# Zero-padding the rotary keys so that a 64-partition score product runs on 128

## The chip, the cores and the metric

The kernel runs on one core of a Trainium2 chip, in one launch. The metric is device time in microseconds. TensorE (PE) multiplies, with a load of its weights for each product (PEld); VectorE (DVE), ScalarE (ACT) and GpSimd (POOL) do the elementwise work, and SyncE (SP) issues most DMAs.

## What is computed

A diffusion backbone of two layers, each with a half-step feed-forward block, token mixing, and a second half-step block. Token mixing adds an mLSTM and a latent attention. The tokens are 256 of context and 256 latent ones. The attention has 8 heads; a head's queries and keys are a part of 128 columns without position and a rotary part of 64 columns, whose keys all heads share. Cut to that:

```
k_rope = _rope(z['a_kr'][:, :, None, :], cos, sin)
k = concatenate([k_nope, broadcast_to(k_rope, (B, T, A_HEADS, A_ROPE))], axis=-1)
q = concatenate([q_nope, _rope(q_rope, cos, sin)], axis=-1)

s = einsum('bqhd,bkhd->bhqk', q, k) * (128 + 64) ** -0.5
pr = softmax(s, axis=-1)
o = einsum('bhqk,bkhd->bqhd', pr, v)
```

Context queries see the 256 context keys; latent queries see all 512. In the last layer only latent queries are computed.

## The kernel before

All tensors lie with features on partitions and tokens along columns. Each operand of a large product is held as two parts, hi (the value in a rounded form, made by ACT) and lo (the rest, made by DVE), and a product is three: hi by hi, lo by hi, hi by lo. Weights come by DMA on SP as units of up to 1024 columns (`unit`), which ACT and DVE split into such parts.

Token mixing is `mix(l, after)`. The program order is written by generators: `mla()` yields between the steps of the attention, `mlstm()` between those of the other mixer, and a `Feed` puts steps of other products between them and draws the elementwise chains an operation at a time (`pump`). The framework's scheduler then sets the final order on each engine and picks which of the 56 work buffers of the pool `act` each tile gets.

The rotary keys are made once per layer, ahead of the attention: 64 rows are copied twice into the tile `krz`, once to each half of the partitions; `rope_gen` rotates the latent columns in place, and `split_gen` makes `kr`, a pair of tiles hi and lo over 128 partitions and 512 columns. For the queries, `head_parts` makes per head one tile over 128 partitions: the head's own half holds the hi part, the other half the lo part.

`scores(p, hd, s)` in `mla()` makes two blocks of scores (`sc`) for pair p, head hd of the pair and stream s, each of five products in one group (L1159). The first three are on the 128 columns without position. The fourth takes the query tile over 128 partitions with `kr[0]`, so hi and lo of the queries meet the keys' hi part in one product. The fifth takes the keys' lo part and must meet only the hi part of the queries, so both operands are cut to the head's own 64 partitions:

```
rp = slice(64 * hd, 64 * hd + 64)
steps = [(qh, kh), (ql, kh), (qh, kl), (qr[hd], kr[0]), (qr[hd][rp], kr[1][rp])]
```

Behind the scores come a maximum (`mx`, DVE L1163), an exponential and a scaling (`pr`, ACT L1168 and L1172), the transposes (`pT`, PE L1182), their split, and the product with the values (`ho`). There are 16 such jobs in layer 0 and 8 in layer 1. The scores' maxima share DVE with the gate chain of the mLSTM, the splitting of weights (`wl`, L226) and the convolution's taps. The taps read tiles `cpd`, whose edges POOL sets to zero (L684, L685).

Of the kernel before, what the change touches and what calls it, by code (L numbers as in the profile page):

```python
# [8 lines left out]
F32 = mybir.dt.float32  # L9
F32R = mybir.dt.float32r  # L10
# [6 lines left out]
P = 128  # L17
# [106 lines left out]
def body(ctx, tc, A):  # L124
# [29 lines left out]
    def put_aside():  # L154
        """The residual leaves its room to the token mixing, which needs it only at its end."""
        for j in range(KB):
            nc.sync.dma_start(aside[:, j, :], xs[j])
# [31 lines left out]
    def pair(n):  # L189
        """Room for the two parts of an operand of n columns."""  # L190
        if n <= HALF:
            t = act(F32R, "hl")
            return t[:, :n], t[:, HALF : HALF + n]
        return act(F32R, "hi")[:, :n], act(F32R, "lo")[:, :n]

    def split(src, n, hi_lo=None, scale=None):
        """src, or scale * src, as two parts."""
        hi, lo = pair(n) if hi_lo is None else hi_lo
        if scale is None:
            S.activation(hi, src, AF.Copy)  # L200
            V.tensor_tensor(lo, src, hi.bitcast(F32), ALU.subtract)
        else:
            S.activation(hi, src, AF.Copy, scale=scale)
            V.scalar_tensor_tensor(lo, src, scale, hi.bitcast(F32), ALU.mult, ALU.subtract)
        return hi, lo
# [5 lines left out]
    def load(dst, src):  # L211
        """On the SP queue, and at the start behind what the first norm needs."""
        with tc.issue_after(behind.pop(0)) if behind else nullcontext():
            nc.sync.dma_start(dst, src)
# [15 lines left out]
    def units(keys, n, kb):  # L230
        """A weight cut along its rows: a list of (hi, lo) [P, N] blocks."""
        res = []
        for key in keys:
            hi, lo = unit(key, n, kb)
            for k in range(kb):
                res.append((hi[:, k, :], lo[:, k, :]))
        return res

    def mm3(ps, lhs, rhs, lsl=slice(None), rsl=slice(None), late=False):
        """late: the second parts of rhs come last, as they are not there yet."""  # L240
        n = len(lhs)
        steps = [(k, *p) for k in range(n) for p in ((0, 0), (1, 0), (0, 1))]
        if late:
            steps.sort(key=lambda t: t[2])
        for i, (k, a, b) in enumerate(steps):
            TE.matmul(ps, lhs[k][a][:, lsl], rhs[k][b][:, rsl], start=i == 0, stop=i == 3 * n - 1)  # L246

    def mmu(parts, keys, n, kb, rhs, flip=False, turns=True):
        """Several products with one weight, cut along its rows into units: each
        unit serves all products before the next one is needed. parts: (out, slice  # L250
        of the unit's columns or of rhs' columns when flip, whether it is the first
        one of its bank: those of one bank form one group, as its first product clears
        the bank's marks). turns: the products take turns, block by block."""
        k0, nk = 0, len(rhs)
        for key in keys:
            hi, lo = unit(key, n, kb)
            order = [(k, i) for k in range(kb) for i in range(len(parts))]
            if not turns:
                order.sort(key=lambda t: t[1])
            for _, group in groupby(order, lambda t: t[0] if turns else 0):  # L260
                for k, i in group:
                    ps, sl, fresh = parts[i]
                    end = i + 1 == len(parts) or parts[i + 1][2]
                    (a, al), (b, bl) = (hi[:, k, :], lo[:, k, :]), rhs[k0 + k]
                    if flip:
                        (a, al), (b, bl) = (b[:, sl], bl[:, sl]), (a, al)
                    else:
                        a, al = a[:, sl], al[:, sl]
                    first, final_ = fresh and k0 + k == 0, end and k0 + k == nk - 1
                    TE.matmul(ps, a, b, start=first, stop=False)  # L270
                    TE.matmul(ps, a, bl, start=False, stop=False)  # L271
                    TE.matmul(ps, al, b, start=False, stop=final_)  # L272
                yield
            k0 += kb
# [5 lines left out]
    # The engine holds one set of functions at a time: Tanh is in one, Ln in another,  # L280
    # Exp in both.
# [12 lines left out]
    def tanh_half(out, src):  # L294
        """2 sigmoid(x) - 1"""
        held[0] = "tanh"
        S.activation(out, src, AF.Tanh, scale=0.5)

    def silu2(out, src):
        """2 x sigmoid(x)"""  # L300
        tanh_half(out, src)
        V.scalar_tensor_tensor(out, out, 1.0, src, ALU.add, ALU.mult)

# [7 lines left out]
    def silu_rows():  # L311
        """Twice the silu of the two conditioning vectors on every partition, in halves."""
# [9 lines left out]
    def ada_first():  # L322
        """Shift and scale of the first norm, before anything else can run."""
        # both parts of both vectors side by side, as one operand of four columns
# [67 lines left out]
    class Ada:  # L392
        """Modulation blocks, fed into other work; loads run some blocks ahead."""
# [10 lines left out]
        def run(self, frac):  # L404
            """Until this share of the blocks is done."""
# [15 lines left out]
    def newton(r, ss, n, width, t=None):  # L421
        """One step that takes r = rsqrt(ss / width + EPS) to float32's accuracy."""
# [5 lines left out]
    def rstd_of(sq_sum, n, width):  # L428
        """sq_sum: to be summed over the partitions, and over its list."""
# [10 lines left out]
    class Norm:  # L440
        """Sum of squares over the blocks of one stream, added as they come."""
# [32 lines left out]
    def flush():  # L474
        """The norm that a stream still lacks."""
        while pending:
            pending.pop()()
# [5 lines left out]
    def last_blocks(make, rhs, streams, l, g, norms, norm, tail=2):  # L483
        """The 8 output blocks of a product added to the residual; the last ones (tail) by
        streams, so that a stream's norm runs beside the other's products."""
# [89 lines left out]
    def mix(l, after):  # L575
# [12 lines left out]
        class Feed:  # L588
            """Work that stands between the steps of the attentions, whose steps wait
            for each other: products that need no other result soon (step), and the  # L590
            elementwise chains behind them, an operation at a time (pump)."""
# [28 lines left out]
            def advance(self, i):  # L620
                """One step of this item; whether it had one left."""
# [12 lines left out]
            def step(self, n=1, open_=lambda key: True):  # L634
                """n steps of the first items that there is room for."""
# [19 lines left out]
        # two blocks of the queries' width: a bank each, or one for both  # L655
# [13 lines left out]
        def split_gen(jobs, scale=None):  # L669
            """jobs: (source, hi, lo)."""  # L670
# [10 lines left out]
        def conv_start(ps):  # L681
            """The tokens of two segments, each between zeros."""
# [6 lines left out]
        def conv_gen(jobs, scale):  # L689
            """Three taps along the tokens, then silu, then the two parts. jobs: (padded  # L690
            tokens, first weight's column by segment, hi, lo)."""
# [24 lines left out]
        def gate_rows():  # L716
            """Gates of all heads and directions as rows: head h forward at h, backward
            at 32 + h; and what the exponents need of them."""
# [8 lines left out]
        def gate_chain(f, i_, e):  # L727
            rows = lambda t, a=0, b=36: t[a:b, :T]
            yield from log_sigm(rows(f), rows(e))
            # parts that are multiples of 2^-12 add without rounding; the rest is small  # L730
# [52 lines left out]
            # minus the stabiliser, exactly, and its parts for the product that spreads it  # L783
# [17 lines left out]
        def gate_cols():  # L801
            """As columns of tokens."""
# [17 lines left out]
        def log_sigm(f, e):  # L820
            """f becomes log sigmoid(f)."""
# [9 lines left out]
        # latent projections of the attention  # L831
# [22 lines left out]
        def rope_gen(z, c0, then):  # L854
            """In place on the latent columns of z, which start at c0; then the parts."""
# [13 lines left out]
        def head_parts(z, dst):  # L869
            """By head: both parts of the queries one over the other, as the rows of one product."""  # L870
# [40 lines left out]
        def gate2(key, keys, name):  # L911
            """2 sigmoid - 1 of two blocks."""
# [24 lines left out]
        class Head:  # L937
# [97 lines left out]
            def scale(self):  # L1035
# [5 lines left out]
                # a first rsqrt from the bits, then to float32's accuracy  # L1041
# [11 lines left out]
            def turn(self):  # L1053
                """Back to columns of tokens, times the output gate."""
# [91 lines left out]
        def mla():  # L1146
            def scores(p, hd, s):
# [3 lines left out]
                rp = slice(64 * hd, 64 * hd + 64)  # L1151
                (qh, ql), (kh, kl) = qn_[hd], kn[hd]
                steps = [(qh, kh), (ql, kh), (qh, kl), (qr[hd], kr[0]), (qr[hd][rp], kr[1][rp])]
# [88 lines left out]
        kr = pair(T)  # L1242
        rope = rope_gen(z, HALF, split_gen([(z, *kr)]))
# [31 lines left out]
        # merge  # L1275
# [57 lines left out]
def _pack(I):  # L1333
# [65 lines left out]
    # constants of the shapes alone  # L1399
# [36 lines left out]
```

## Time and profile before

| | before |
|---|---|
| median of 3 runs | 2396.31 us (2394.90 to 2396.78) |
| span of the profiled execution, core 0 | 2395.4 us |
| PE busy | 2352.9 us (98%) |
| DVE busy | 1601.3 us (67%) |
| ACT busy | 990.7 us (41%) |
| POOL busy | 171.9 us (7%) |
| HBM traffic | 131 GB/s over the span |

The page gives the profiled execution by its span, from the first to the last instruction; what lies around it is what the times of the runs have beyond that, at most 1.4 us here. PE is busy nearly throughout, but its busy time is a sum over stretches of different kinds, and starts and ends must be read in the rows: matmuls overlap, and their ends are modelled. A start-to-start distance is the time that a product takes in the row of products.

### The profile page before, as it was taken

The page shows a single profiled execution, that of the slowest core. Times are in us where ns is not written, and L with a number is a line of the kernel's source. Part 1 is how long each engine was busy: PE and PEld are TensorE (multiplying, and loading weights), DVE is VectorE, ACT ScalarE, POOL GpSimd, SP SyncE. Part 2 cuts the span into 40 slices and gives each one's busy share as a digit, 9 for nine tenths or more (in the row PEclk, how much of TensorE's full clock was granted, in tenths as well). Part 3 has the DMA queues.
Part 4 walks back from the last instruction along what each step waited for, and adds up shares of the span by engine and source line. Part 5 has one row for each costly group of instructions (what it writes and reads, how often), then busy time and mean ns, then how long its engine had stood idle before and what let it go on. Part 6 is the DMA issues. An engine that isn't in the chain of part 4 may idle for free.

```text
span 2395.4 us, 34542 instructions
## 1 busy us (share of the span) xinstructions
PE 2352.9 (98%) x13170; PEld 2008.8 (84%) x13170; DVE 1601.3 (67%) x3375; ACT 990.7 (41%) x1630; POOL 171.9 (7%) x384
## 2 busy tenths in 40 slices
PE   8999999999999999999999999999999999999998
PEld 4888888888888888888888898888887799999998
DVE  7887777786477654479986663334357867776665
ACT  6322223556555442242222242222245654555443
POOL 1112110000010000012231000000000000000000
PEclk9999999999999999999999999999999999999999
DMA  8656444211122222355585322232232223354563
GB/s 317 204 168 228 150 146 158 86 56 53 62 80 71 72 79 97 132 194 186 202 299 187 115 101 99 78 116 89 76 103 80 99 80 106 103 170 152 175 209 117
DMA packets 101251, 316.93 MB, mean 132 GB/s; under 512 B 13150, under 2 KB 15454, under 8 KB 101086
## 3 DMA queue, kind: packets, MB, share of 16 engines
q1 hardware_dynamic: 80606, 247.61, 30.3%
q0 software_dynamic: 20480, 67.13, 8.1%
q8 instruction: 103, 1.69, 0.3%
q14 instruction: 62, 0.51, 0.1%
HBM read 311.54 MB, written 3.15 MB: 131 GB/s over the span
## 4 chain that ended last, share of the span: by engine, by line
PE 95%; DVE 3%; ACT 2%; issue 1%; DMA 0%; DVEq 0%; SPq 0%; ACTq 0%
PE dn L246 20%; PE pa L270 5%; PE pb L270 5%; PE pb L272 5%; PE pa L272 5%; PE pa L271 5%; PE pb L271 5%; PE p L270 4%; PE p L271 4%; PE p L272 4%; PE sc L1159 2%; PE pv L246 2%; PE pa L246 2%; PE pb L246 2%; PE k L270 1%; PE k L271 1%
## 5 line engine op out<-in xcount | busy, mean ns | idle before, releaser
L224 ACT ACTIVATE wh<-st 128x1024 fp32r<-128x1024 f32 (+1 forms) x484 | 471.3, 976 | 945.3 <-PE pb L271 253.6
L226 DVE TENSOR_TENSOR wl<-st,wh 128x1024 fp32r<-128x1024 f32 (+1 forms) x484 | 540.4, 1119 | 374.2 <-ACT wh L224 370.3
L246 PE MATMUL dn<-hi,wl 128*128 128x512 f32 (+1 forms) x674 | 247.7, 367 | 0.0
L246 PE MATMUL dn<-hi,wh 128*128 128x512 f32 (+1 forms) x674 | 247.3, 368 | 0.0
L246 PE MATMUL dn<-lo,wh 128*128 128x512 f32 (+1 forms) x674 | 246.5, 366 | 0.0
L270 PE MATMUL pa<-hh,wh 128*128 128x512 f32 (+1 forms) x640 | 234.4, 366 | 0.0
L270 PE MATMUL pb<-hh,wh 128*128 128x512 f32 (+1 forms) x640 | 234.4, 366 | 0.0
L272 PE MATMUL pa<-hh,wl 128*128 128x512 f32 (+1 forms) x640 | 234.2, 366 | 0.0
L272 PE MATMUL pb<-hh,wl 128*128 128x512 f32 (+1 forms) x640 | 234.2, 366 | 0.0
L271 PE MATMUL pa<-hl,wh 128*128 128x512 f32 (+1 forms) x640 | 234.2, 366 | 0.0
L271 PE MATMUL pb<-hl,wh 128*128 128x512 f32 (+1 forms) x640 | 234.2, 366 | 0.0
L364 POOL DMA_DIRECT2D ada<-ada x256 | 137.2, 537 | 736.0 <-PE dn L246 216.1
L271 PE MATMUL p<-hl,wh 128*128 128x256 f32 (+1 forms) x536 | 179.6, 335 | 0.0
L270 PE MATMUL p<-hh,wh 128*128 128x512 f32 (+1 forms) x512 | 174.1, 340 | 0.0
L272 PE MATMUL p<-hh,wl 128*128 128x512 f32 (+1 forms) x512 | 172.6, 337 | 0.0
L375 DVE SCALAR_TENSOR_TENSOR ada<-ada,cs 128x512 f32<-128x512 f32 x256 | 166.3, 684 | 0.0
L246 PEld LDWEIGHTS dn<-hi,wh 128*128 128x128 f32 x674 | 126.7, 188 | 23.4
L246 PEld LDWEIGHTS dn<-hi,wl 128*128 128x128 f32 x674 | 126.6, 188 | 22.7
L246 PEld LDWEIGHTS dn<-lo,wh 128*128 128x128 f32 x674 | 126.7, 188 | 22.4
L270 PEld LDWEIGHTS pb<-hh,wh 128*128 128x128 f32 x640 | 120.2, 188 | 22.0
L272 PEld LDWEIGHTS pb<-hh,wl 128*128 128x128 f32 x640 | 120.0, 188 | 22.1
L272 PEld LDWEIGHTS pa<-hh,wl 128*128 128x128 f32 x640 | 120.0, 188 | 22.1
(361 smaller groups left out, 4979.1 us busy)
## 6 DMA issues: line engine op xcount, KB each, us to landing
st<-wall SPq DMA_DIRECT2D x340, 512.0 KB, 3.3
ada<-ada POOLq DMA_DIRECT2D x256, 256.0 KB, 3.4
st<-wall SPq DMA_DIRECT2D x72, 384.0 KB, 2.9
st<-wall SPq DMA_DIRECT2D x64, 320.0 KB, 2.9
ada<-ada SPq DMA_DIRECT2D x32, 256.0 KB, 5.4
x<-xT SPq DMA_DIRECT2D x8, 256.0 KB, 5.8
cb<-cc SPq DMA_DIRECT2D x8, 256.0 KB, 5.8
aside<-x SPq DMA_DIRECT2D x8, 256.0 KB, 2.0
```

The costliest lines, as they stand in the source:

```text
L224: S.activation(hi[:, :n], st[:, :n], AF.Copy)
L226: V.tensor_tensor(lo[:, :n], st[:, :n], hi[:, :n].bitcast(F32), ALU.subtract)
L246: TE.matmul(ps, lhs[k][a][:, lsl], rhs[k][b][:, rsl], start=i == 0, stop=i == 3 * n - 1)
L270: TE.matmul(ps, a, b, start=first, stop=False)
L271: TE.matmul(ps, a, bl, start=False, stop=False)
L272: TE.matmul(ps, al, b, start=False, stop=final_)
L364: nc.gpsimd.dma_start(st, ada[ADA[l, g] + j, :, q * 512 : (q + 1) * 512])
L375: V.scalar_tensor_tensor(o, st, 0.5, cb[s, q], ALU.mult, ALU.mult, accum_out=dst)
L1159: TE.matmul(ps[qb], a[:, c], b[:, :nk], start=i == 0, stop=i == len(steps) - 1)
```

## The change

The keys' lo part is kept once for each of the two heads of a pair, in a tile of 128 partitions whose own half holds it and whose other half is zero. The fifth product then takes the whole query tile and that whole key tile; the zeros take away the queries' lo part. The tile of the hi part stays one. The subtraction that makes the lo part becomes two on 64 partitions, and POOL sets the two other halves to zero ahead of it, once per layer. One tile more of the pool `act` is held through the attention. (The diff also drops comments, so lines shift.)

```diff
 def scores(p, hd, s):
-    rp = slice(64 * hd, 64 * hd + 64)
     (qh, ql), (kh, kl) = qn_[hd], kn[hd]
-    steps = [(qh, kh), (ql, kh), (qh, kl), (qr[hd], kr[0]), (qr[hd][rp], kr[1][rp])]
+    steps = [(qh, kh), (ql, kh), (qh, kl), (qr[hd], kr[0]), (qr[hd], kr[1][hd])]
...
-    kr = pair(T)
-    rope = rope_gen(z, HALF, split_gen([(z, *kr)]))
+    kr = act(F32R, "krh")[:, :T], [act(F32R, "krl")[:, :T] for _ in range(2)]
+    own = slice(0, 64), slice(64, 128)
+
+    def key_parts():
+        S.activation(kr[0], z, AF.Copy)
+        yield
+        for hd in range(2):
+            V.tensor_tensor(kr[1][hd][own[hd]], z[own[hd]], kr[0][own[hd]].bitcast(F32), ALU.subtract)
+            yield
+
+    for hd in range(2):
+        G.memset(kr[1][hd][own[1 - hd]].bitcast(F32), 0.0)
+    rope = rope_gen(z, HALF, key_parts())
     next(rope)
```

On PE, in layer 0 at the first latent score job, the order stood so before (`p` is a projection by head, the unnumbered hi and lo are the keys' and queries' rotary parts):

```order
L271 MATMUL p_4339<-hl,wh 128x512
L1159 MATMUL sc<-hi 128x512 [waits DVE_49]
L1159 MATMUL sc<-lo,hi 128x512
L1159 MATMUL sc<-hi 128x512
L1159 MATMUL sc<-lo,hi 128x512
L272 MATMUL p_4339<-hh,wl 128x512
```

And with the change:

```order
L271 MATMUL p_4343<-hl,wh 128x512
L1158 MATMUL sc<-krh,hi 128x512 [waits DVE_49]
L1158 MATMUL sc<-krl,hi 128x512 [waits Pool_49]
L1158 MATMUL sc<-krh,hi 128x512
L1158 MATMUL sc<-krl,hi 128x512
L272 MATMUL p_4343<-hh,wl 128x512
```

Nothing moved; the fifth product (krl) now also waits for POOL's memset. The order on PE is the same throughout, but for one pair of projections in layer 1.

On POOL, ahead of the token mixing of layer 0, where the edges of the first convolution's tiles are set, the difference reads:

```order
 L364 DMA ada<-ada 128x512 [waits DMASW7_49,DVE_49]
-L684 MEMSET cpd 128x2 [waits DMAHW2_49,DVE_49]
-L685 MEMSET cpd 128x2
-L684 MEMSET cpd 128x2 [waits DMAHW6_49,DVE_49]
+L1253 MEMSET krl 64x512 [waits PE_49,Pool_49]
+L1253 MEMSET krl 64x512 [waits PE_49]
+L684 MEMSET cpd 128x2 [waits DMAHW6_49,DVE_49,Pool_49]
+L685 MEMSET cpd 128x2
+L684 MEMSET cpd 128x2 [waits DMAHW3_49,DVE_49]
 L685 MEMSET cpd 128x2
```

Two memsets, each with a wait for a buffer that PE read last, come in ahead of the padding memsets.

On DVE, at the end of the rotary keys of layer 0:

```order
 L865 TENSOR_TENSOR krz<-krz,rt 128x256 [waits DVE_49]
 L843 TENSOR_TENSOR sq<-sq 128x512 [waits Activation_49]
-L676 TENSOR_TENSOR lo<-krz,hi 128x512 [waits Activation_49]
+L1249 TENSOR_TENSOR krl<-krz,krh 64x512 [waits Activation_49]
+L1249 TENSOR_TENSOR krl<-krz,krh 64x512
 L226 TENSOR_TENSOR wl<-st,wh 128x1024 [waits DMAHW0_49,PE_49,Activation_49]
```

One subtraction became two, ahead of the same split of a weight.

## Rows read from the trace of the kernel before

**Rows 1.** The page: the chain that ended last, share of the span by engine.
```profile
PE 95%; DVE 3%; ACT 2%; issue 1%; DMA 0%; DVEq 0%; SPq 0%; ACTq 0%
```

**Rows 2.** Line L1159: count, duration min/median/max in ns, first and last start, forms.
```profile
L1159 PE MATMUL sc<-lo,hl x16: 491/492/502, 1841.1 to 1951.3; 64*128 64x512 f32 x16
```

**Rows 3.** PE in order of time: start us, us, engine, line, instruction, weights, moving.
```profile
485.71 0.40 PE L1159 MATMUL sc<-hi 128*128 128x512 f32 x1
486.04 0.50 PE L1159 MATMUL sc<-lo,hi 64*128 64x512 f32 x1
486.47 0.50 PE L1159 MATMUL sc<-hi 128*128 128x512 f32 x1
486.90 0.50 PE L1159 MATMUL sc<-lo,hi 64*128 64x512 f32 x1
487.33 0.51 PE L272 MATMUL p<-hh,wl 128*128 128x512 f32 x1
487.67 0.39 PE L270 MATMUL p<-hh,wh 128*128 128x512 f32 x1
487.90 0.28 PE L1159 MATMUL sc<-hi,qnh 128*128 128x256 f32 x1
```

**Rows 4.** The same, just behind, with 256 columns.
```profile
488.14 0.28 PE L1159 MATMUL sc<-lo,qnh 128*128 128x256 f32 x1
488.26 0.28 PE L1159 MATMUL sc<-hi 128*128 128x256 f32 x1
488.47 0.39 PE L1159 MATMUL sc<-lo,hi 64*128 64x256 f32 x1
488.79 0.38 PE L1159 MATMUL sc<-hi,qnh 128*128 128x256 f32 x1
```

**Rows 5.** Weight loads in order of time; in brackets the idle time before, and its releaser.
```profile
486.47 0.19 PEld L1159 LDWEIGHTS sc<-hi 128*128 128x128 f32 x1 [0.25 <-issue]
```

**Rows 6.** PE in order of time at the 64-row product of 587.11.
```profile
587.11 0.38 PE L1159 MATMUL sc<-lo 64*128 64x256 f32 x1
587.11 0.46 PE L811 MATMUL pt<-consts,pk 64*128 64x64 f32 x4
```

**Rows 7.** POOL and DVE in order of time: padding memset; the keys' lo part.
```profile
429.42 0.11 POOL L684 MEMSET cpd<- 128x2 f32 x1 [64.20 <-DVE hl L465]
...
462.54 0.69 DVE L676 TENSOR_TENSOR lo<-krz,hi 128x512 fp32r<-128x512 f32 x1
```

**Rows 8.** DVE in order of time; then busy time of PE, PEld, DVE, ACT, POOL, clock.
```profile
486.58 0.69 DVE L1163 TENSOR_REDUCE mx<-sc 128x1 f32<-128x512 f32 x1 [3.35 <-PE sc L1159]
487.44 0.69 DVE L1163 TENSOR_REDUCE mx<-sc 128x1 f32<-128x512 f32 x1 [0.17 <-PE sc L1159]
...
488.89 0.42 DVE L1163 TENSOR_REDUCE mx<-sc 128x1 f32<-128x256 f32 x1 [0.17 <-PE sc L1159]
489.87 0.42 DVE L1163 TENSOR_REDUCE mx<-sc 128x1 f32<-128x256 f32 x1 [0.56 <-PE sc L1159]
...
500.00:525.00 25.00, 25.00 (x167) 22.49 (x166) 24.27 (x51) 15.72 (x33) 1.97 (x4) 1.00 0.10 32
```

**Rows 9.** PE in order of time: its waits for DVE and ACT in these stretches.
```profile
532.52 0.50 PE L1159 MATMUL sc<-hi 128*128 128x512 f32 x1 [0.34 <-DVE hi L876]
...
544.09 0.66 PE L1182 MATMUL pT<-consts,pr 128*128 128x128 f32 x4 [0.22 <-ACT pr L1168]
...
1881.46 1.12 PE L1182 MATMUL pT<-consts,pr 128*128 128x128 f32 x4 [3.68 <-ACT pr L1168]
```

**Rows 10.** DVE in order of time, layer 1.
```profile
1844.32 0.69 DVE L1163 TENSOR_REDUCE mx<-sc 128x1 f32<-128x512 f32 x1 [0.92 <-PE sc L1159]
...
1845.87 0.69 DVE L1163 TENSOR_REDUCE mx<-sc 128x1 f32<-128x512 f32 x1 [0.27 <-PE sc L1159]
```

**Rows 11.** A gap of PE, and the stretch around it (clock third from the end).
```profile
1032.72 0.38 PE L246 MATMUL pa<-hh,wh 128*128 128x256 f32 x1 [2.16 <-ACT hh L464]
...
1000.00:1040.00 40.00, 37.84 (x221) 33.53 (x221) 24.61 (x50) 15.24 (x30) 6.42 (x12) 0.96 0.38 132
```

## The prediction

> **What bounds the kernel now.** I read the chain of waits first: 95% of the chain that ended last is PE work [rows 1], in a span of 2395.4 us. So time comes off where PE's own sequence gets shorter, as long as nothing else is late there. Next I read the line of the score products. Each of the 24 score jobs (16 in layer 0, 8 in layer 1) makes two score blocks, and each block ends with one product on 64 partitions. That makes 48 such products, in three groups of 16, of which one stands in [rows 2]. Then I read PE in order of time around the first of them. What counts is the distance from one start to the next, since the ends are modelled. Two full products of 512 columns start 0.23 us apart (487.67 to 487.90). Around the two 64-row ones the distances are 0.33, 0.43, 0.43, 0.43 and 0.34 [rows 3], together 1.96 where five times 0.23 would be 1.15. The excess is 0.81 for two, 0.40 each. With 256 columns the undisturbed distance is 0.12, and there the 64-row product makes it 0.21 and then 0.32 [rows 4]: 0.29 over two distances, and with the third, taken as 0.10 from the last distance above, 0.39. I take 0.39. The price does not grow with the columns, so it is a change of shape, not work. The weight loads show which: the load of the full product behind a 64-row one starts only with its own product, after 0.25 us in which the load side waited for nothing that the profile shows [rows 5]; elsewhere loads of 0.19 us run under the product before. One change into 64 rows and one out each expose a load, 0.2 us.
>
> **What the change removes.** All 48 products run on 128 rows with the same columns, and PE's order stays the same around them; only the shape changes. If the zero half costs no more than any other operand, each takes 0.23 or 0.12 us like its neighbours, and 48 x 0.39 = 18.7 us of PE time go. One of them, at 587.11, is followed at once by four 64-row transposes, which start in the same hundredth of a microsecond [rows 6]; these keep their change of shape in and out, so 47 count: **18.3 us** is the most that can go.
>
> From the other side: the Trainium skill, "TensorE: Matmul & The Clock Gate", section "Why this matters for your kernels", says that a single matmul on 32 rows takes the same time as one on 128, and that few rows pay only when several tiles run at once. By that the change would remove 0. The trace disagrees, with 0.43 against 0.23 us.
>
> **What it adds.** Per layer, the one subtraction of 128 partitions (0.69 us on DVE) becomes two of 64 partitions. I price each at 0.69, by the same 512 columns [rows 7], so 0.69 us more, and between 0 (two halves as one) and 0.69. In both layers DVE afterwards still stands without work until PE's first scores: 3.35 us in layer 0 [rows 8], 0.92 in layer 1 [rows 10]. That covers it; without the cover it would be 0.7 us per layer. Two memsets of 64 x 512 on POOL stand ahead of the small memsets of the convolution's padding. POOL had been without work for 64.20 us there [rows 7], and the first 64-row product comes 56 us later, so I cost them at nothing. If their buffers came free late, the padding memsets would queue behind them, then ACT's copies into the padded tiles, then DVE's taps; a delay that uses up such a distance I don't see. One more of the 56 work buffers is held through each token mixing; its cost is between 0 and the slower rival below, and I take 0, as PE's waits are few.
>
> **What DVE gives back.** PE is not alone everywhere. From 489.87 us on DVE is nearly full: 24.27 of 25 us from 500 to 525 [rows 8]. At 532.52 PE already waits 0.34 us for DVE, at 544.09 0.22 us for an ACT result behind it, and at 1881.46 3.68 us [rows 9]. Where DVE ends last, PE's gain only lengthens the wait, and what stays is the time by which DVE itself starts sooner:
> - Layer 0 up to 532: eight products, 8 x 0.39 = 3.1 us on PE. DVE waited for their results 0.17, 0.17 and 0.56 us [rows 8]; these waits go, and its first reduction (486.58) comes 0.2 us sooner, as the second product both starts and ends 0.1 sooner. DVE gains 1.1 us. So **1.1** stays, and the wait at 532 grows from 0.34 to some 2.3 us.
> - From 532 to 544: four products, 1.6 us; the wait at 544 shows no room, and DVE was partly waiting in between, so I take half, **0.8** (between 0 and 1.6).
> - From 544 to the end of layer 0's attention: twenty, less the one at 587: 19 x 0.39 = **7.4**. No wait of PE stands there.
> - Layer 1 up to 1881: six products, 2.3 us. DVE's waits for them are 0.92 and 0.27 us [rows 10]; DVE gains 1.2, so **1.2** stays and the wait of 3.68 becomes some 4.8.
> - Layer 1 behind it: ten products, 3.9 us. DVE and ACT stand in another order there after the change, and are nearly full for four of these ten. Between 2.3 (the last six alone) and 3.9; I take **3.1**.
>
> Sum: 1.1 + 0.8 + 7.4 + 1.2 + 3.1 = 13.6 us. The longer wait at 532 has a price of its own. After PE's gap of 2.16 us at 1032.72, the granted clock of the stretch from 1000 to 1040 is 0.96, so 0.04 x 40 = 1.6 us of clock are lost: for some 3 us the lower level, 1.2 GHz, was granted [rows 11]. A gap of 2.3 us at 532 probably brings the same loss, of which half falls away, as a slower PE arrives at 544 when DVE is ready: 0.8 net. **13.6 - 0.8 = 12.8 us.** The profiled execution would go from 2395.4 to 2382.6. The median of the runs shown, 2396.31, lies 0.9 above that span, so the forecast for the median is **2383.5 us**.
>
> **Rivals.**
> - All of it arrives. DVE's fullness moves with PE, nothing new is waited for, no clock is lost: 2396.3 - 18.3 = 2378.0. For it: most of PE's waits in these stretches are under half a microsecond. Against it: at 532 and 1881 DVE is the last, and it cannot run ahead of its own order. Chance 0.11.
> - DVE and the clock eat more. Nothing stays of the 12 products up to 544 (4.7) and of the first ten of layer 1 (3.9), and two stretches at the lower clock come in addition (3.2): 18.3 - 4.7 - 3.9 - 3.2 = 6.5, so 2389.8. For it: the full DVE; against it: DVE did wait for PE in both places [rows 8, 10]. Chance 0.10.
> - The change does not do what it says: what costs is not the 64 rows but the fifth product's own operands (a load of weights that the product before has just used, a key tile shared by the heads). Then 128 rows pay the same, the gain is 0, and the time 2396.3. Against it: the delay falls as well on the product behind, which at 487.33 is a projection with other operands [rows 3]. The Trainium skill's rule above would give the same time; the trace does not bear it out. Chance 0.04.
> - Slower, by buffers: with one of 56 held longer, a softmax tile in a score job waits for an older tile's last reader, and the transposes behind it, in PE's order, wait as at 1881 for 3.68 us [rows 9]. 18.3 / 3.68 = 5: more than five such waits in 24 jobs lose all; in every second job it is 12 x 3.68 - 18.3 = 26 us more, 2422. For it: one buffer less must make some tile wait for an older reader. Against it: PE's waits in these stretches are few and short, so tiles come free in time, with room to spare. Chance 0.03.
>
> **How the numbers follow.** The forecast's own case, 2380 to 2387, has 0.72. The range takes in the first two rivals at their values, **2377.8 to 2390.0**; outside are no change, slower, and the far sides of those two. Differences under 0.2%, 4.8 us, are about what a measurement of this kernel cannot tell from no change. Faster by more: 0.72 + 0.11 + nearly all of 0.10 = 0.92. Within 0.2%: 0.04 and the rest of the second rival, 0.05. Slower: 0.03.
>
> **What would show it.** In the changed kernel's trace the products on the zero-padded keys should have 128 partitions, start 0.23 or 0.12 us apart like their neighbours, and their weight loads should begin under the product before. PE's wait for DVE near 531 should be 2 to 2.5 us, with the granted clock at half for some 3 us behind it; the one near 1880 should be 4.5 to 5 us. The memsets should lie before 430 and 1800 us with nobody waiting for them. The prediction is wrong if the distances stay at 0.3 to 0.4 (no change of shape was paid for), or if new waits of softmax tiles on PE or POOL appear.

## The result and the profile after

The changed kernel takes 2383.32 us (median of 5 runs, 2382.99 to 2383.56). The kernel before, run beside it, takes 2396.31 us (median of 5 runs, 2394.90 to 2397.06). The ratio is 0.9945, with a 95% interval of 0.9933 to 0.9957: **13 us faster**, 0.2 us from the forecast of 2383.5 and inside its range. The span of the profiled execution is 2381.9 us, where 2382.6 was forecast.

The page of the changed kernel, its busy times:

```profile
PE 2336.3 (98%) x13170; PEld 2011.6 (84%) x13170; DVE 1601.8 (67%) x3377; ACT 989.5 (42%) x1630; POOL 174.1 (7%) x388
```

PE issues the same 13170 products and is busy 16.6 us less. PE's share of the chain [rows 1] hardly moved, from 95 to 94%; such a row tells where to look and not how much can come off.

PE in order of time, changed kernel, at the place of [rows 3] and then at that of [rows 4]; columns as there:

```profile
485.14 0.40 PE L1158 MATMUL sc<-krh,hi 128*128 128x512 f32 x1
485.38 0.40 PE L1158 MATMUL sc<-krl,hi 128*128 128x512 f32 x1
485.62 0.39 PE L1158 MATMUL sc<-krh,hi 128*128 128x512 f32 x1
485.84 0.39 PE L1158 MATMUL sc<-krl,hi 128*128 128x512 f32 x1
486.07 0.39 PE L272 MATMUL p<-hh,wl 128*128 128x512 f32 x1
486.30 0.40 PE L270 MATMUL p<-hh,wh 128*128 128x512 f32 x1
...
487.01 0.28 PE L1158 MATMUL sc<-krl,hi 128*128 128x256 f32 x1
487.13 0.28 PE L1158 MATMUL sc<-hi,qnh 128*128 128x256 f32 x1
```

The distances from start to start are now 0.22 to 0.24 us throughout, where 0.33 to 0.43 stood. From the first score product to the second projection behind the last 64-row one it is 1.16 us instead of 1.96. With 256 columns the distance is 0.12. The two traces can be laid side by side product by product, as PE's order is the same. The way from the product ahead of a 64-row one to the second product behind it is then shorter by 0.37 to 0.41 us at 36 of the 48 places, and the median is 0.39 with 512 columns and with 256. The twelve others are places where two such ways overlap or a wait changed, and the one at 587.11, which gains nothing.

The weight loads of the same place, changed kernel (start, duration):

```profile
485.15 0.19 PEld L1158 LDWEIGHTS sc<-krl,hi 128*128 128x128 f32 x1
485.38 0.19 PEld L1158 LDWEIGHTS sc<-krh,hi 128*128 128x128 f32 x1
```

The load of the product of 485.38 starts at 485.15, so 0.23 us ahead of it and under the product before; the idle 0.25 us of [rows 5] is gone. Summed up over the line, the view of the score products says how long PE's sides stood idle ahead of them without waiting for anything that the profile shows. For the kernel before it is this row (us, times), and the changed kernel has no such row:

```profile
issue: 13.8, 45
```

What was added costs PE nothing. POOL and DVE in order of time, changed kernel:

```profile
411.60 1.10 POOL L1253 MEMSET krl<- 64x512 f32 x2 [46.95 <-PE dn L246]
```

```profile
461.94 1.39 DVE L1249 TENSOR_TENSOR krl<-krz,krh 64x512 fp32r<-64x512 f32 x2
...
485.82 1.29 DVE L1162 TENSOR_REDUCE mx<-sc 128x1 f32<-128x512 f32 x2 [3.18 <-PE sc L1158]
...
487.61 0.74 DVE L1162 TENSOR_REDUCE mx<-sc 128x1 f32<-128x256 f32 x2
488.27 0.41 DVE L733 TENSOR_SCALAR gfh<-gf 36x512 f32<-36x512 f32 x1
```

The two half subtractions take 1.39 us, twice the 0.69 of the whole one [rows 7], and in layer 0 DVE still stands 3.18 us without work ahead of its first maximum. In layer 1 the time comes out of a wait of DVE for ACT just behind the subtractions, 2.47 us where 3.17 stood. The memsets are done 16.6 us before the padding ones in layer 0 and 20 us before them in layer 1; only POOL's own next memset stands behind them. Of [rows 8], the waits of 0.17, 0.17 and 0.56 us are gone. The operation behind these maxima, which starts at 488.27 here, started later in the kernel before (its DVE in order of time):

```profile
490.21 0.41 DVE L733 TENSOR_SCALAR gfh<-gf 36x512 f32<-36x512 f32 x1
```

PE's waits in the attention, changed kernel, beside [rows 9]:

```profile
497.20 0.39 PE L246 MATMUL ho<-hi 128*128 128x256 f32 x1 [1.46 <-ACT hi L672]
...
530.33 0.50 PE L1158 MATMUL sc<-krh,hi 128*128 128x512 f32 x1 [0.73 <-DVE hi L876]
531.86 0.47 PE L270 MATMUL p<-hi,wh 128*128 128x512 f32 x1 [0.33 <-DVE lo L676]
540.68 1.17 PE L1181 MATMUL pT<-consts,pr 128*128 128x128 f32 x8 [0.44 <-DVE vl L676]
...
1868.85 0.66 PE L1181 MATMUL pT<-consts,pr 128*128 128x128 f32 x4 [4.70 <-ACT pr L1167]
1870.46 0.79 PE L246 MATMUL kn<-hi,wh 128*128 128x512 f32 x1 [0.96 <-ACT pr L1167]
```

Two of these stood in the kernel before too, smaller (its PE in order of time):

```profile
499.34 0.38 PE L246 MATMUL ho<-hi 128*128 128x256 f32 x1 [0.71 <-ACT hi L672]
...
1882.96 0.79 PE L246 MATMUL kn<-hi,wh 128*128 128x512 f32 x1 [0.38 <-ACT pr L1168]
```

So part of what PE gained turned into longer waits: 0.75 + 0.39 + 0.33 + 0.22 = 1.7 us in layer 0, and 1.02 + 0.58 = 1.6 us in layer 1.

The wait in layer 1 has a price in clock besides. PE's busy time in the 10 us from its end on, in the kernel before (wait of 3.68 us) and then in the changed one (4.70 us); the columns are stretch, length, PE busy and products, granted clock (1.00 is 2.4 GHz, 0.50 is 1.2 GHz), DMA share, GB/s:

```profile
1881.46:1891.46 10.00, 9.62 (x30) 0.72 0.18 63
```

```profile
1868.85:1878.85 10.00, 9.04 (x29) 0.66 0.21 76
```

That is 2.8 us of clock lost before and 3.4 after, 0.6 more.

**Where the 13.5 us of the span come from.** The same product of PE was looked up in both traces at the edges of the stretches that the prediction named (us from the start of the span). The names are those of the traces; `cq`, `pa`, `kn`, `s` and `nps` are products of other steps and serve as marks:

| product on PE | before | after | gained in the stretch up to it | predicted |
|---|---|---|---|---|
| first `cq` with a wait, layer 0 | 416.55 | 415.97 | 0.58 | 0 |
| score product that waits for DVE | 532.52 | 530.33 | 1.61 | 1.1 |
| first score product behind the waiting `pT` | 544.51 | 541.61 | 0.71 | 0.8 |
| projection behind the last scores of layer 0 | 625.44 | 615.39 | 7.15 | 7.4 |
| `pa` with a wait | 1407.54 | 1397.29 | 0.20 | 0 |
| first `kn` with a wait, layer 1 | 1827.49 | 1816.17 | 1.07 | 0 |
| `pT` that waits for ACT | 1881.46 | 1868.85 | 1.29 | 1.2 |
| `v` behind the last scores | 1951.72 | 1936.24 | 2.87 | 3.1 |
| `s` with a wait | 2027.73 | 2012.11 | 0.14 | 0 |
| last `nps` | 2385.58 | 2372.05 | -2.09 | 0 |

The five stretches of the change give 13.63 us. The prediction had 13.6 for them, and 12.8 with the clock loss of 0.8 that it put behind the wait at 532. All else sums to -0.10, where it had nothing.

Two entries outside the change's places, 1.07 and -2.09, come in the main from stretches at the lower of the two clock levels, 1.2 GHz. Each is shown by the gap of PE ahead and by the busy time of PE in the 10 us around. The kernel before:

```profile
1407.54 0.39 PE L246 MATMUL pa<-hh,wh 128*128 128x256 f32 x1 [0.98 <-ACT hh L464]
...
1406.00:1416.00 10.00, 8.97 (x51) 0.83 0.31 116
...
2027.73 0.39 PE L246 MATMUL s<-qh,kh 128*128 128x256 f32 x1 [2.06 <-ACT qh L672]
...
2026.00:2036.00 10.00, 8.27 (x41) 1.00 0.33 107
```

The changed kernel, at the same two products:

```profile
1397.29 0.39 PE L246 MATMUL pa<-hh,wh 128*128 128x256 f32 x1 [0.95 <-ACT hh L464]
...
1396.00:1406.00 10.00, 9.05 (x64) 1.00 0.42 139
...
2012.11 0.39 PE L246 MATMUL s<-qh,kh 128*128 128x256 f32 x1 [2.06 <-ACT qh L672]
...
2010.00:2020.00 10.00, 7.94 (x34) 0.83 0.31 107
```

One such stretch went and another came, each 0.17 x 10 = 1.7 us of clock; 0.6 us in the first entry and 0.4 in the second have a cause that was not traced. The gaps ahead are nearly as long in both kernels. Neither belongs to the rotary product, and after_again below shows that such stretches differ between two executions of one and the same kernel.

### The profile page after: what moved, and what is told of

The parts are those of the page before. It is cut to its first block, busy times and chain, and to the rows that moved or that the text cites. A ratio compares the mean times of both kernels' runs of the same rounds, so it can differ in the third digit from the quotient of the medians.

```text
span 2381.9 us, 34548 instructions
## 1 busy us (share of the span) xinstructions
PE 2336.3 (98%) x13170; PEld 2011.6 (84%) x13170; DVE 1601.8 (67%) x3377; ACT 989.5 (42%) x1630; POOL 174.1 (7%) x388
## 4 chain that ended last, share of the span: by engine, by line
PE 94%; DVE 3%; ACT 2%; issue 1%; DMA 0%; DVEq 0%; SPq 0%; ACTq 0%
PE dn L246 20%; PE pb L271 5%; PE pa L271 5%; PE pa L272 5%; PE pb L270 5%; PE pa L270 5%; PE pb L272 5%; PE p L270 4%; PE p L271 4%; PE p L272 4%; PE pv L246 2%; PE pa L246 2%; PE pb L246 2%; PE sc L1158 2%; PE k L270 1%; PE k L271 1%
## 5 line engine op out<-in xcount | busy, mean ns | idle before, releaser
L270 PEld LDWEIGHTS pa<-hh,wh 128*128 128x128 f32 x640 | 120.4, 188 | 21.7
```

## The experiments

### Is the price one of shape, or of 64 rows, or of operands?

**pair64**: the kernel before, with the fifth products of both blocks put last in the job, so that two 64-row products are neighbours wherever nothing of another chain is fed between them (17 of 24 jobs).

```diff
-    for i, (a, b) in enumerate(steps):
-        TE.matmul(ps[qb], a[:, c], b[:, :nk], start=i == 0, stop=i == len(steps) - 1)
+    for i, (a, b) in enumerate(steps[:-1]):
+        TE.matmul(ps[qb], a[:, c], b[:, :nk], start=i == 0, stop=False)
+for qb in range(2):
+    a, b = steps[-1]
+    TE.matmul(ps[qb], a[:, c], b[:, :nk], start=False, stop=True)
```

> The kernel before, with the two 64-row products of a job put at the job's end, so that they can follow each other: 17 of the 24 jobs then have them in a row on PE, in 7 something stands between. Theory (the price is the change of shape, 0.39 us for in and out): 48 - 17 = 31 changes in and out are left, 17 x 0.39 = 6.6 us less PE time, of which DVE's lateness leaves some three quarters: about 5 us, 2391. In the trace the second of two neighbouring 64-row products starts 0.23 us (512 columns) or 0.12 us (256) behind the first. Rival (each 64-row product pays, as its weights are loaded late): the second starts 0.43 or 0.31 us behind the first, and the time stays at 2396.

Measured: 2393.38 us (2390.23 to 2394.12), the kernel before on that chip 2397.57; ratio 0.998 [0.9971, 0.9989], 4.2 us less, where about 5 were forecast. PE in order of time in this kernel, at the place of [rows 3]:

```profile
486.34 0.63 PE L1159 MATMUL sc<-hi 128*128 128x512 f32 x2
486.90 0.73 PE L1163 MATMUL sc<-lo,hi 64*128 64x512 f32 x2
487.56 0.50 PE L272 MATMUL p<-hh,wl 128*128 128x512 f32 x1
487.89 0.39 PE L270 MATMUL p<-hh,wh 128*128 128x512 f32 x1
```

From 486.34 to 487.89 five products take 1.55 us, 0.40 more than 5 x 0.23; alone, the two 64-row products cost 0.81. The second neighbour pays for its columns alone. The idle time of the score products says the same. In this kernel the 64-row products have a line of their own, whose row is

```profile
issue: 7.2, 20
```

With 0.7 us in 3 times at the line of the other score products that makes 7.9 us in 23 times, where 13.8 in 45 stood. So the 64 rows can stay, if they stand side by side; what costs is going in and out.

**zero128, zero64, zero64x2**: the changed kernel, with one more product of zero weights put into each of 69 groups of the last products (`dn`): on 128 rows, on 64, and two in a row on 64. 48 of them have 512 columns and 21 have 256.

```diff
+zk = cp.tile([P, P], F32R, name="zk")
+G.memset(zk.bitcast(F32), 0.0)
...
         TE.matmul(ps, lhs[k][a][:, lsl], rhs[k][b][:, rsl], start=i == 0, stop=i == 3 * n - 1)
+        if junk and i == 4:
+            for _ in range(1):
+                TE.matmul(ps, zk[:128], rhs[0][0][:128, rsl], start=False, stop=False)
```

(64 for 128 in the second kernel, and `range(2)` besides in the third.)

> The changed kernel with one product more in each of 69 groups of the feed-forward's and the token mixing's last products (48 of 512 columns, 21 of 256): weights of zero over 128 rows, which add nothing to the result. It is the base for the next two. Both theories: 48 x 0.234 + 21 x 0.117 = 13.7 us more PE time, 2397.

> The same 69 products on 64 rows. Theory (in and out cost 0.39 us whatever the columns, in a place where nothing but PE is late): 69 x 0.39 = 26.9 us over the one with 128 rows, 2424. Rival (few rows cost nothing by themselves; what cost in the scores were their operands): 2397, like the one with 128 rows.

> Two such 64-row products in a row at each of the 69 places (66 of them neighbours on PE). Theory (a change of shape in and one out per place): the second adds only its columns, 13.7 us, and 3 x 0.39 where the two are apart: 2424 + 14.9 = 2439. Rival (each 64-row product pays 0.39): 2424 + 13.7 + 26.9 = 2465.

Measured on one chip: 2395.96 us (2394.62 to 2397.35), 2421.39 (2420.60 to 2423.31) and 2437.88 (2435.68 to 2438.84); the kernel before there 2397.20, ratios 0.9994 [0.9985, 1.0004], 1.0101 [1.0086, 1.0116] and 1.0167 [1.0152, 1.0182]. The 128-row products cost 12.6 us against the changed kernel's 2383.32 on another chip; their columns alone are 48 x 0.23 + 21 x 0.12 = 13.6. The 64-row ones cost 25.4 us more: 25.4 / 69 = **0.37 us each**. The second neighbour adds 16.5, of which 13.6 are its columns. PE in order of time in the second kernel, then in the third:

```profile
1776.07 0.40 PE L248 MATMUL dn<-hi,wl 128*128 128x512 f32 x1
1776.40 0.50 PE L251 MATMUL dn<-hi,zk 64*128 64x512 f32 x1
1776.84 0.50 PE L248 MATMUL dn<-lo,wh 128*128 128x512 f32 x1
1777.17 0.39 PE L248 MATMUL dn<-hi,wh 128*128 128x512 f32 x1
```

```profile
1786.16 0.39 PE L248 MATMUL dn<-hi,wl 128*128 128x512 f32 x1
1786.48 0.72 PE L251 MATMUL dn<-hi,zk 64*128 64x512 f32 x2
1787.12 0.50 PE L248 MATMUL dn<-lo,wh 128*128 128x512 f32 x1
1787.47 0.39 PE L248 MATMUL dn<-hi,wh 128*128 128x512 f32 x1
```

One: 1.10 us for three distances, 0.41 over 3 x 0.23. Two: 1.31 for four, 0.39 over 4 x 0.23. zero128 and zero64 differ in nothing but the rows: weights of the same tile meet the same columns. So the rival of the operands falls.

The Trainium skill, "TensorEngine Tiling (Array Packing)", section "Key Properties", says that a change of the tiling mode drains TensorE. The runs agree with it and put a price on it, 0.37 us in and out. The Trainium skill's rule that the prediction weighed, that few rows take the time of many, does not hold for a single product between others of 128 rows.

### Does the gain divide over the layers as summed?

**only_l0** and **only_l1**: the change in one layer alone. (The making of the key tiles, not shown, goes by `WIDE` as well.)

```diff
+WIDE = (True, False)
...
-steps = [(qh, kh), (ql, kh), (qh, kl), (qr[hd], kr[0]), (qr[hd], kr[1][hd])]
+steps = [(qh, kh), (ql, kh), (qh, kl), (qr[hd], kr[0]),
+         (qr[hd], kr[1][hd]) if WIDE[l] else (qr[hd][rp], kr[1][rp])]
```

> The change in layer 0 alone. The sum of the prediction gives 1.1 + 0.8 + 7.4 = 9.3 us without any clock term, so 2387.0; the layer-0 terms as read from the changed kernel's trace are 9.5. Rival (the gain of the two layers is not additive, as stretches at the lower clock come and go with it): off that by 1.5 us or more, with one such stretch more or fewer in the trace than in the kernel before.

> The change in layer 1 alone. The sum of the prediction gives 1.2 + 3.1 = 4.3 us, so 2392.0, and PE's wait at 1881 grows from 3.68 to some 4.8 us. Rival (not additive, by stretches at the lower clock): off that by 1.5 us or more, with one such stretch more or fewer in the trace.

Measured on the chip of pair64: 2386.10 us (2385.39 to 2388.08), ratio 0.9950 [0.9934, 0.9967], and 2394.44 (2392.27 to 2395.62), ratio 0.9982 [0.9973, 0.9991]; so 11.5 and 3.1 us, where 9.3 and 4.3 were summed. Together they make 14.6, and that is what the changed kernel with 54 buffers (below) gains on the same chip, 2397.57 to 2383.01: the gains of the two layers add up.

In layer 0 alone, the `pa` of 1407.54 us starts at 1397.17, 10.4 us sooner; 0.6 of it was there at the first `cq` (415.96), ahead of any change. That leaves 9.8 us gained, where 9.3 was summed. The rest of the 11.5 comes behind it, where the stretch at the lower clock near 1410 us is missing in this kernel. In layer 1 alone, the `s` of 2027.73 us starts at 2024.35, 3.4 us sooner, though the first `cq` of layer 0, ahead of any change, starts 1.2 us later (417.78): 4.6 us gained, where 4.3 was summed. Then part of it goes again. PE in order of time, only_l1:

```profile
2024.35 0.39 PE L247 MATMUL s<-qh,kh 128*128 128x256 f32 x1 [2.06 <-ACT qh L673]
```

The granted clock from 2022 to 2032 us is 0.83: the stretch at the lower clock that the changed kernel has there, and the kernel before not, is in this one too. Layer 0 alone does not have it: its `s` starts at 2016.72 behind the same gap of 2.06 us, and the granted clock from 2016 to 2026 is 1.00. By these rows the layers' sums hold within 0.5 us; the times of the runs are 1 to 2 us off them, by this clock and by the start. The wait at 1881 became 4.60 us in layer 1 alone, where 4.8 was expected, and stayed at 3.58 in layer 0 alone.

### Does the tile that is held longer cost anything?

**buf54**: the changed kernel with 54 buffers in the pool `act` instead of 56.

```diff
-ap_ = ctx.enter_context(tc.tile_pool(name="ap", bufs=56))
+ap_ = ctx.enter_context(tc.tile_pool(name="ap", bufs=54))
```

> The changed kernel with 54 work buffers in place of 56: the suspected cost of the one tile more that the change holds, taken twice again. Theory (buffers cost nothing here): 2383.3 within 1.5 us, and PE's waits in the attention as in the changed kernel. Rival (buffers are short): PE waits for ACT or DVE that wait for a PE reader, at 0.5 to 4 us each, and more than 3 us slower than the changed kernel.

Measured: 2383.01 us (2382.07 to 2385.14), ratio 0.9936 [0.9921, 0.9951], and the waits of the changed kernel within a tenth (1.46 at 497.64, 0.82 at 530.85, 4.63 at 1868.83). Buffers are not what stood between 13 and 18 us.

### Can what DVE keeps back be had?

Three versions of the changed kernel try it. **slow43** draws the mLSTM's gate chain at every fourth or third step instead of every third or second:

```diff
-SLOW = (3, 2)
+SLOW = (4, 3)
```

> The changed kernel, with the chain of the mLSTM's gates drawn more slowly between the attention's steps: at every 4th and 3rd operation (layer 0, layer 1) in place of every 3rd and 2nd. Theory (DVE's fullness at the start of the attention, with the gate chain in it, is what gives back 3.1 - 1.6 us at 530, and the wait of 4.70 at 1869): PE's waits at 497 to 541 and at 1869 shrink, together by 2 to 5 us, and the time falls to 2379 to 2382. Rival (these waits are the latency of softmax and transposes, not DVE's load): they stay, 2383; or the gates are ready late, and the mLSTM's start waits: slower than 2383.

Measured: 2389.09 us (2384.03 to 2390.51), ratio 0.9962 [0.9948, 0.9976], where 2379 to 2382 was forecast. By the two ratios that is some 4 us slower than the changed kernel's 0.9945 on another chip, with intervals that overlap. The wait near 1869 falls from 4.70 to 2.21 us and that at 530 goes, but PE now waits for DVE elsewhere: 1.62 us at 547.20, and in layer 1 1.25 us at 1892.79, with a granted clock of 0.50 from 1894 to 1896, and 1.38 us here (slow43's PE in order of time):

```profile
1890.81 0.50 PE L1158 MATMUL sc<-krh,hl 128*128 128x512 f32 x1 [1.38 <-DVE hl L876]
```

**pool4** moves four subtractions of the gate chain per layer (36 rows, 512 columns) from DVE to POOL; here one of them:

```diff
-V.tensor_tensor(rows(pk1), rows(ih), rows(bh), ALU.subtract)
+G.tensor_tensor(rows(pk1), rows(ih), rows(bh), ALU.subtract)
```

**nobl** takes the four DVE sums over the gates' small parts per layer out:

```diff
-scan(bl, f, zero, d, cols, 0.0, ALU.add, ALU.add)
-yield
```

**after_again** is the changed kernel once more, on the chip of these two.

> The changed kernel with four subtractions of 36 x 512 in the gate chain (0.68 us each on DVE) moved to POOL, per layer. Theory (DVE's work in the first 50 us of the attention is what gives PE's gain back): DVE has 2.7 us less there; PE's wait at 1869 falls from 4.70 to some 2 us, those of 497 to 541 from 2.96 together to about 1, and the time to 2379 to 2381.5. Rival (as in the slower chain, the lateness comes up again at another place, or DVE now waits in its own order for POOL): 2383 or more, with waits of the same sum elsewhere.

> The changed kernel without the running sums of the gates' small parts: four scans of 4 x 256 (0.68 us each on DVE) per layer are left out, so the exponents lack those parts. It takes as much off DVE as the four subtractions on POOL, and nobody waits for POOL. Theory: as there, 2379 to 2381.5, with the wait at 1869 down to some 2 us. Rival (the waits are latency of softmax and transposes): the wait at 1869 stays over 4 us and the time at 2383.

> The changed kernel as it is, on the same chip as the two above, to compare them with: 2383.3, with waits of 1.5 and 4.7 us at 497 and 1869 as in its first profile. The rival that its gain hangs on where stretches at the lower clock fall would show as another set of such stretches and a time that differs by 1.5 us or more.

Measured: 2382.34 us (2381.20 to 2384.26), 2383.94 (2381.30 to 2384.33) and 2383.72 (2382.64 to 2385.18), against 2397.34 for the kernel before; ratios 0.9936 [0.9921, 0.9951], 0.9939 [0.9922, 0.9955] and 0.9941 [0.9927, 0.9956]. The three cannot be told apart, and 2379 to 2381.5, the forecast for the first two, was missed by both. PE's waits in pool4, in order of time, and its busy time from the wait in layer 1 on:

```profile
509.94 0.38 PE L246 MATMUL ho<-lo,hi 128*128 128x256 f32 x1 [2.10 <-DVE lo L676]
...
1869.84 0.66 PE L1181 MATMUL pT<-consts,pr 128*128 128x128 f32 x4 [1.25 <-ACT pr L1167]
1873.66 0.50 PE L246 MATMUL kn<-hi,wh 128*128 128x512 f32 x1 [1.47 <-DVE vl L676]
...
1869.84:1879.84 10.00, 8.46 (x42) 1.00 0.31 107
```

The wait of 4.70 us is down to 1.25, and behind it the granted clock is 1.00 where the changed kernel has 0.66. In its place stand 1.47 at 1873.66 and 2.10 at 509.94, the latter with a granted clock of 0.83 in the 10 us behind it. In nobl the waits from 530 to 541 are gone, and 0.50 at 545.92 and 0.71 at 548.54 come; the large one keeps 3.74. PE's waits of more than 0.15 us in the two attentions (470 to 630 and 1815 to 1960 us) sum to 12.4 us in after_again, 12.6 in pool4 and 11.4 in nobl. Where DVE's work is lightened or spread differently in a full stretch, another operation of its order is late. No version beat the changed kernel by more than its interval.

One wait did not move: the one at 497, for ACT's `hi`, is 1.46 us in slow43, pool4 and nobl as in the changed kernel. ACT is busy for 9.65 of the 9.80 us ahead of it in the changed kernel (from 487.70 on) and in pool4 (from 487.95 on) alike. So lightening DVE does not help there; ACT's own row is full.

The second profile of the changed kernel, after_again, has PE's waits as in the first (1.45 at 497.78, 4.70 at 1870.36), but for one more of 1.20 us at 1823.11, and another set of stretches at the lower clock. Its PE's busy times around the `pa` of 1397.75, whose gap is 0.95 us as before, and around the `kn` of 1817.82:

```profile
1396.00:1406.00 10.00, 8.96 (x53) 0.83 0.39 131
```

```profile
1817.00:1827.00 10.00, 7.21 (x41) 1.00 0.22 73
```

In the first profile these were 1.00 at the one place and 0.83 (1816 to 1826) at the other, behind gaps of the same lengths, 0.95 and 1.55 us. The spans are 2381.9 and 2382.0 us, so the rival's other half, a time that differs by 1.5 us or more, did not come.

## Why the prediction was right

- **The price of one 64-row product** was read off the trace of before as 0.39 us, one change of shape in and one out. The changed kernel's distances and loads show it gone; laid side by side, the two traces give 0.39 again; zero64 gives 0.37 for a product of its own, and zero64x2 and pair64 show that neighbours share one price. This was the step on which all hung.
- **47 of 48.** The four transposes behind the product of 587.11 [rows 6] kept their change of shape: in the changed kernel they start at 580.06, 0.21 us behind a score product of 256 columns, and the projection behind them only at 580.45. The way around this product is not shorter than before.
- **What DVE keeps back.** The sum by stretches, 13.6 us, came out as 13.63. The single terms hold within some 0.5 us, and their misses partly cancel (+0.5, -0.1, -0.25, +0.1, -0.2). The largest miss is the stretch up to 532, 1.61 instead of 1.1. DVE's first operation behind the first maxima, 490.21 us in the kernel before, starts at 488.27 in the changed one, 1.94 sooner; 0.58 of it had come before. So DVE gained 1.36 us there: two reductions of 0.69 us in a row start 0.60 apart (1.29 us for both), and each wait that goes brings 0.09 more than its length. That DVE keeps back the rest at 530 to 541 and at 1869, with ACT behind it, is shown by the releasers of the grown waits, and by slow43, pool4 and nobl, which change DVE's work and move these waits. It is not shown for the largest part in layer 0, the 0.75 us at 497: this wait is for ACT, whose row is full, and the three kernels leave it as it is. For the stretch up to 532 the prediction weighed DVE alone.
- **The wait at 532** was to grow from 0.34 to 2.3 us in one place. It came in parts: 0.75 at 497, 0.39 at 530, 0.33 and 0.22 behind. This step failed, and with it the next; what stayed by 532 was 1.61 and not 1.1.
- **The clock** was to fall behind that wait, for 0.8 us net. It did not; the busy times of PE in the changed kernel have the full clock, 2.4 GHz, all along:

```profile
485.00:530.00 45.00, 43.07 (x279) 1.00 0.13 43
530.00:545.00 15.00, 13.90 (x70) 1.00 0.40 135
```

  In its place one stretch at 1.2 GHz left the place near 1410 us and one came near 2014. With the rest outside the five stretches this nets to -0.10 us. The prediction charged no clock to the wait at 1881, where the loss was 2.8 us already and grew by 0.6. That the median was met to 0.2 us is partly luck: the span was 0.7 us shorter than forecast, and the median came near only because it lies 1.4 us above the span, where 0.9 was taken. Other stretches at the lower clock can put a time 1 to 2 us off, as in only_l1: 3.1 us gained, where 4.3 was summed.
- **Additions at nothing.** Memsets, the second half subtraction and the held tile cost nothing that can be measured; buf54 shows it for the tile, with two buffers fewer than the changed kernel has. The prediction's cover for the subtraction in layer 1 was misread: the 0.92 us [rows 10] stand ahead of the third maximum, and the first two (1842.07 us) followed other work of DVE without a wait. What took the 0.7 us up was the wait for ACT just behind the subtraction.
- **The rivals.** "All of it arrives" (2378.0) fell to the grown waits: at 0.37 to 0.39 each, 47 products are 17.4 to 18.3 us, and less 1.7 and 1.6 of waits and 0.6 of clock that is 13.5 to 14.4; 13.6 were found. "DVE and the clock eat more" (2389.8) had nothing staying up to 544, where 2.3 us stayed. "Operands" (2396.3) fell to zero64, and "buffers" (2422) to buf54.

## What to carry to other kernels

Read the price of a PE instruction from start to start and over its neighbours too: a product on fewer rows can cost more than its own time, as the loads around it lose their cover. If zeros on the other partitions can make the shapes equal, or if the odd shapes can stand side by side, the change is paid once or never. And sum a saving by stretches, with what the next engine can follow: here almost 5 of 18 us were lost, most of them in longer waits for DVE and ACT and in the clock behind one of these waits, and rearranging DVE's work only moved its lateness.

## What was not expected of the hardware

- A second 64-row product behind a first one costs little more than its columns (16.5 us for 69, of which 13.6 are columns), and the price of the change is the same with 512 columns and with 256 (0.39 us).
- On DVE, 64 partitions take as long as 128 (1.39 us for two halves, 0.69 for the whole), and two maxima that last 0.69 us each start 0.60 apart when nothing is waited for (1.29 us for both). The two halves did not, and no run shows why.
- A gap of PE of 2.06 us was followed by a granted clock of 1.00 in the kernel before and in only_l0, and by a stretch at 1.2 GHz in the changed kernel and in only_l1; gaps of 0.98 and 0.95 us differ likewise. The program alone does not decide it: two executions of the changed kernel differ behind equal gaps of 0.95 and of 1.55 us. One such stretch is 1.7 us of clock. What decides it stays open: no run varied it alone.
